# A hybrid decoder block: squares of the tokens without GpSimd, a row of factors spread by products, one value operand in another buffer, two value pieces loaded later

## The chip, the core and the metric

The kernel runs on one core of one Trainium2 chip. The metric is device time in microseconds (us) from start to end of one execution, as the median of several runs. The core has five engines that work side by side, each in the order of its own program: TensorE (PE in the profile; its weight loads are PEld), VectorE (DVE), ScalarE (ACT), GpSimd (POOL) and SyncE (SP), which issues most of the transfers.

## The reference

One decoder block on 2048 tokens of width 1024, all in float32. Cut to what matters:

```python
xn = rmsnorm(h, pre_gain[i])
z = xn @ w_in[i]
q, k, v, fl, g_attn, x_lru, g_lru = jnp.split(z, SPLIT_POINTS, axis=-1)
o_attn = forgetting_attention(q, k, v, fl + b_f[i])          # 8 heads of 128, causal
y_attn = rmsnorm(o_attn, attn_out_gain[i]) * jax.nn.silu(g_attn)
o_lru = rg_lru(causal_depthwise_conv(x_lru, conv_w[i], conv_b[i]), ...)
y_lru = rmsnorm(o_lru, lru_out_gain[i]) * jax.nn.silu(g_lru)
mix = jnp.concatenate([y_attn, y_lru], axis=-1) @ w_out[i]
h = h + rmsnorm(mix, post_gain[i])
e = rmsnorm(p[i] @ w_ple[i], ple_gain[i])                     # per-layer embedding
gate = jax.nn.sigmoid(h @ w_ple_gate[i] + b_ple_gate[i])
h = h + gate * e
```

## The kernel before

Every large product is computed as three products of split operands: a high half (ScalarE copies the source into a rounded type) and a low half (VectorE or GpSimd subtracts the high half from the source). `mm3` (lines 63 to 70) issues high by high, high by low, low by high. The input products are further made by a Strassen-like scheme of seven products on half-size blocks: `XH[i]`, `XL[i]` are the seven token operands, and a `Unit` makes the seven weight operands.

The first third of the program is written as a calendar of slots. `plan(slot, phase, f)` puts a step in a slot; within a slot the phases run in the order LOAD, COMBINE, PREP, JOB, MUL, GATE, STORE, and within a phase in the order of planning. A slot holds about one group of products for TensorE. Since each engine works through its own instructions in order, the calendar fixes what stands behind what on each engine and on the queue of SP.

The opening of the calendar (slots -4 to 30) does this:

- Warming products on a zeroed tile (lines 804 to 808) keep TensorE busy until the first data come.
- The embedding: `ple_load` and `ple_split` bring the per-layer inputs in eight pieces; `embed_mul` makes the 16 tiles of `p @ w_ple`, one tile of twelve products in each of slots 0 to 15; `embed_squares` (ScalarE) sums their squares, and `embed_out` (lines 787 to 796) multiplies each with the row of factors `ple_gain`, held in `pgb` on all 128 partitions. `pgb` is filled by one broadcast load of 512 KB (line 825), which stands in SP's queue between the pieces of tokens. A tile's pair of PSUM banks comes from three such pairs (`bank2`), so tile t needs tile t-3 to be done with.
- The scales of the tokens: `stage_piece` loads the first half of the tokens in eight pieces of 512 KB. `square` (lines 671 to 686) squares them, `add` sums them, `fold` halves the sum, `column_sums` makes sums over partitions by products with ones, `column_roots` takes the roots, `scale_diagonals` and `spread_scales` spread them by a product, and `normalize` multiplies the tokens. There are two groups of 512 tokens, n = 0 and 1. One square of four in each group runs on GpSimd, the others on ScalarE; the additions run on VectorE.
- `plan_operand` splits the token operands, and `differ` makes four of them by subtraction.
- The value unit (begins at slot `VA` = 16, two slots for each of its seven products in the order 0, 5, 1, 2, 3, 4, 6). `plan_weights` (from line 318) gives each of its 14 half operands a buffer out of a ring of five (`op`) and a slot: `sums` (additions and subtractions of weight blocks, on GpSimd), `high` (ScalarE), `low` one slot later in COMBINE (VectorE, for operands 0 and 5 GpSimd), `keep` (stored for the second half of the tokens). The raw weights have a ring of four buffers (`wq`). `plan_v` has the products and what VectorE and ScalarE do with the results.
- At slot `LA` = 30 the units of the recurrent branch begin (their products are the lines with `bank<-XH,op`), and after them the same scheme goes on for some 350 slots in all.

Then attention begins with another calendar: `at(before, slot, f)` and `at(after, slot, f)` place side steps ahead of and behind the work of a slot. In each slot TensorE turns a block of probabilities (`turn_probs`, line 1324), ScalarE and VectorE split it (line 54, line 60), and TensorE multiplies it with the values. Keys and values come in pieces: `load_piece` loads one, `split_piece` splits it on ScalarE and GpSimd. Two value pieces of the first head (numbers 5 and 7, blocks 8 to 15) are loaded at slots 5 and 7 and split at slots 9 and 11; they are first used at slots 27 and 43.

Of the kernel before, what the change touches and what calls it, by code (L numbers as in the profile page):

```python
# [16 lines left out]
P = 128  # L17
# [19 lines left out]
NC = 7  # L37
RAW0 = 5
LOAD, COMBINE, PREP, JOB, MUL, GATE, STORE = range(7)
# [34 lines left out]
def hymba_kernel(ctx: ExitStack, tc: tile.TileContext, x, xT, pT, w_p, w_v, w_o, w_ple, w_pg,  # L74
# [170 lines left out]
    class Unit:  # L245
# [27 lines left out]
        def sums(self, i, hf):  # L273
            n = self.cols
            a11, a12, a21, a22 = self.raws(hf)
            sub = lambda o, x, y: nc.gpsimd.tensor_tensor(out=o, in0=x, in1=y, op=ALU.subtract)
            if i == 1 and self.v or i == 2 and not self.v:
                self.S[1, hf] = wp.tile([P, WT // 2], F32, name="ws", bufs=2)[:, :n]
                nc.gpsimd.tensor_tensor(out=self.S[1, hf], in0=a21, in1=a22, op=ALU.add)
            if i == 2:  # L280
                self.S[2, hf] = self.S[1, hf] if self.v else wp.tile([P, WT // 2], F32, name="ws", bufs=2)[:, :n]
                sub(self.S[2, hf], self.S[1, hf], a11)
            elif i == 3:
                sub(self.S[2, hf], a12, self.S[2, hf])
            elif i == 4:
                sub(a21, a11, a21)
# [5 lines left out]
        def high(self, i, hf):  # L292
            n = self.cols
            op = wp.tile([P, WT], F32R, name="op", bufs=NOP)
            nc.scalar.activation(op[:, :n], self.source(i, hf), AF.Copy)  # L295
            self.ops[i, hf] = op[:, :n], op[:, n:2 * n], op
# [17 lines left out]
    def plan_weights(u, lead=4):  # L314
# [4 lines left out]
        for i in u.prep:  # L319
            for hf in halves:  # L320
                end = u.use(i) + u.halves - 1
                s = max(op_ring.free(), u.use(i) - lead)
                if i == (1 if u.v else 2):
                    s = max(s, ws_ring.ends[-1] + 2 if ws_ring.ends else s)
                op_ring.take(s, end)
                if u.use(i) - s < 2:
                    print("late operand", u.kind, u.h, i, hf, u.use(i) - s)
                starts[i, hf] = s
                if i in (1, 2, 3, 4):
                    plan(s - 1, PREP, lambda i=i, hf=hf: u.sums(i, hf))  # L330
                plan(s, PREP, lambda i=i, hf=hf: u.high(i, hf))
                plan(s + 1, COMBINE, lambda i=i, hf=hf: u.low(i, hf))
                plan(min(s + 2, end), STORE, lambda i=i, hf=hf: u.keep(i, hf))
            if i == 3:
                ws_ring.take(s, s + 1)
        for n in range(4 if u.v else 2):
# [10 lines left out]
            if min(users) - s < 2:  # L347
                print("late raw", u.kind, u.h, n, min(users) - s)
            plan(s, LOAD, lambda n=n: u.load_raw(n))

    fetched = [0]
# [318 lines left out]
    def square(p, n, c, eng):  # L670
# [12 lines left out]
        else:  # L683
            nc.gpsimd.tensor_tensor(out=o, in0=src, in1=src, op=ALU.mult)
        if c:
            plan(now[0] + (1 if eng == "act" else 2), COMBINE, lambda: add(a, a, o))

# [99 lines left out]
    def embed_out(tb):  # L787
        eo = E["o", tb] = (te.tile([P, D], F32, name="eo", bufs=3) if 4 <= tb % 7 else
                           v_tile(("u1", "u5", "o11", "o12", "", "", "", "u1", "o11", "u5", "o12",
                                   "", "", "", "u5", "o12")[tb])[:, :D])  # L790
        b, n = flat(tb), 512 if tb >= RAW0 else 0
        if n:
# [12 lines left out]
    nc.vector.memset(warm, 0.0)  # L805
    b = sbank()
    for _ in range(16):
        nc.tensor.matmul(b, lhsT=warm[:, :P], rhs=warm, start=True, stop=True)
    open_stage("sgA")
    open_right("vpA", vp)  # L810
    plan(-4, LOAD, lambda: ple_load(0))
    for j in range(2):
# [3 lines left out]
    plan(-3, LOAD, lambda: ple_load(1))  # L816
    plan(-3, LOAD, lambda: ple_load(2))
    for n in range(2):
        for kh in range(2):
            if (n, kh) == (1, 0):  # L820
                plan(-2, LOAD, lambda: ple_load(3))
            for k in (0, 2):
                plan(n - 3, LOAD, lambda n=n, kh=kh, k=k: stage_piece(0, n, kh, k))
            if n == 0 and kh == 0:
                plan(-3, LOAD, lambda: nc.sync.dma_start(out=pgb, in_=rows[1:2, :].broadcast_to([P, D])))
    plan(-3, PREP, lambda: ple_split(0))
# [10 lines left out]
    plan(60, JOB, embed_roots)  # L837
    for n, when in enumerate(((0, 1, 1, 2), (3, 3, 4, 5))):
        for c in range(4):
            plan(when[c], JOB, lambda n=n, c=c: square(0, n, c, "pool" if c == 1 else "act"))  # L840
        plan(3 + 3 * n, JOB, lambda n=n: fold(0, n))
# [10 lines left out]
    for k in (0, 2):  # L852
        for i, t in ((1, 13), (2, 16), (4, 19), (6, 21)):
            plan(t + k // 2, JOB, lambda i=i, k=k: differ(i, k, 2, nc.vector))
# [9 lines left out]
    plan_operand(4, 22, "dve")  # L864
    plan_operand(6, 24, "dve")

# [548 lines left out]
    for n, (h, g) in enumerate(stages):  # L1415
        at(before, max(t0[n] - 4, t0[n - 1] + 10) if n else t0[n] + 1, lambda h=h, g=g, n=n: load_gate(h, g, units[n]))
    for p_, a in ((5, 9), (7, 11)):
        at(before, a - 4, lambda p_=p_: load_piece(0, p_))
        at(after, a, lambda p_=p_: split_piece(0, p_))
# [405 lines left out]
    def plan_gate(n):  # L1825
# [67 lines left out]
        plan(s - 2, LOAD, load_e)  # L1893
        if n >= RAW0:
            plan(s + 1, JOB, lambda: tt(u.et[:, :512], u.et[:, :512], G_.egain, ALU.mult))
# [88 lines left out]
```

## Time and profile before

| | us |
|---|---|
| median of three runs | 2088.6 |
| lowest, highest run | 2084.8, 2089.59 |
| the profiled execution | 2089.28 |
| its span | 2087.5 |
| TensorE busy | 2066.8 (99%) |
| VectorE busy | 1620.8 (78%) |
| ScalarE busy | 1148.1 (55%) |
| GpSimd busy | 714.3 (34%) |

Times in the trace count from the start of the span. A line of a timeline has the start, the duration, the engine, the line of the kernel, the operation, `out<-in` by the program's names, the shapes, and in brackets how long the engine stood idle before it and what ended that. TensorE's matmuls overlap, so the distance between two starts counts, not the duration. The clock column (PEclk) is the share of TensorE's full clock that was granted. The opening lies at 0 to 107 us, attention begins near 1046 us.

### The profile page before, as it was taken

How to read it: one execution, taken by the hardware profiler on the slowest of the kernel's cores; microseconds unless marked ns; L12 is line 12 of the kernel's file. 1: busy time of each engine (PE TensorE's matmuls, PEld its weight loads, DVE VectorE, ACT ScalarE, POOL GpSimd, SP SyncE). 2: the span in 40 equal slices, each digit the busy share in tenths (PEclk: the TensorE clock that was granted, in tenths of full speed). 3: DMA queues.
4: the chain of work that ended last, by engine and by line, in shares of the span. 5: the costliest groups of instructions: out<-in, count | busy, mean ns of one | idle time of the engine just before them, and what ended most of it. 6: DMA issues, size and time to landing. Idle time of an engine off the chain costs nothing.

```text
span 2087.5 us, 31241 instructions
## 1 busy us (share of the span) xinstructions
PE 2066.8 (99%) x10602; PEld 1745.4 (84%) x10602; DVE 1620.8 (78%) x2674; ACT 1148.1 (55%) x1839; POOL 714.3 (34%) x617
## 2 busy tenths in 40 slices
PE   9999999999999999999999999999999999999999
PEld 6988888888988898888878888888888888888887
DVE  7977988696759877986378888888885778776676
ACT  6536765344337776874167767777773444452232
POOL 4534555333013335633035665666541000000000
PEclk9999999999999999999999999999999999999999
DMA  8598998987898898779758767777643887665553
GB/s 334 205 331 297 316 348 300 374 313 289 274 279 276 277 274 288 257 251 333 237 183 235 239 215 218 233 231 241 195 149 128 285 254 228 190 218 180 178 174 118
DMA packets 254816, 519.15 MB, mean 249 GB/s; under 512 B 24880, under 2 KB 91712, under 8 KB 254656
## 3 DMA queue, kind: packets, MB, share of 16 engines
q1 hardware_dynamic: 254512, 517.11, 75.5%
q8 instruction: 83, 1.36, 0.3%
q14 instruction: 77, 0.63, 0.1%
q10 hardware_dynamic: 144, 0.05, 0.0%
HBM read 314.81 MB, written 202.25 MB: 248 GB/s over the span
## 4 chain that ended last, share of the span: by engine, by line
PE 91%; DVE 4%; DMA 2%; ACT 1%; issue 1%; SPq 0%; POOL 0%; DVEq 0%; ACTq 0%; POOLq 0%
PE bank L70 15%; PE bank L69 15%; PE bank L68 15%; PE pbank L70 7%; PE pbank L68 7%; PE pbank L69 7%; PE tbank L1324 5%; PE sbank L68 3%; PE sbank L70 3%; PE sbank L69 3%; PE obank L69 3%; PE obank L70 3%; PE obank L68 2%; DMA kvf<-v_d 1%; PE bank L1851 1%
## 5 line engine op out<-in xcount | busy, mean ns | idle before, releaser
L68 PE MATMUL bank<-XH,op 128*128 128x512 f32 x876 | 342.2, 391 | 0.0
L70 PE MATMUL bank<-XH,op 128*128 128x512 f32 x876 | 340.9, 389 | 0.0
L69 PE MATMUL bank<-XL,op 128*128 128x512 f32 x876 | 340.8, 389 | 0.0
L368 DVE TENSOR_TENSOR c<-bank,c 128x512 f32<-128x512 f32 x280 | 186.4, 684 | 109.6 <-PE bank L70 98.4
L60 DVE TENSOR_TENSOR tl<-tbank,th 128x512 fp32r<-128x512 f32 (+1 forms) x320 | 192.4, 607 | 87.1 <-ACT th L54 83.7
L54 ACT ACTIVATE th<-tbank 128x512 fp32r<-128x512 f32 (+1 forms) x320 | 167.7, 530 | 113.0 <-PE tbank L1324 103.7
L69 PEld LDWEIGHTS bank<-XL,op 128*128 128x128 f32 x876 | 164.5, 188 | 34.5 <-issue 0.5
L68 PEld LDWEIGHTS bank<-XH,op 128*128 128x128 f32 x876 | 164.5, 188 | 34.3 <-issue 0.5
L70 PEld LDWEIGHTS bank<-XH,op 128*128 128x128 f32 x876 | 164.5, 188 | 34.0
L1296 ACT ACTIVATE pr<-pr,m 128x1152 f32<-128x1152 f32 (+7 forms) x120 | 148.0, 1233 | 42.2 <-DVE m L1287 41.5
L1324 PE MATMUL tbank<-ident,pr 128*128 128x128 f32 x1062 | 167.3, 273 | 0.0
L152 POOL TENSOR_TENSOR rsm<-rs,mhalf 128x1 f32<-128x1 f32 x16 | 8.7, 543 | 431.5 <-DVE rs L151 431.5
L1324 PEld LDWEIGHTS tbank<-ident,pr 128*128 128x128 f32 x1062 | 130.6, 140 | 27.5
L68 PE MATMUL sbank<-kh,qh 128*128 128x512 f32 (+3 forms) x320 | 136.1, 425 | 2.2 <-DVE m L1287 1.2
L68 PE MATMUL obank<-th,vh 128*128 128x512 f32 (+1 forms) x320 | 123.5, 386 | 0.8 <-ACT th L54 0.8
L295 ACT ACTIVATE op<-wq 128x512 fp32r<-128x512 f32 (+1 forms) x96 | 60.1, 630 | 114.5 <-PE bank L70 79.8
L69 PE MATMUL obank<-tl,vh 128*128 128x512 f32 (+1 forms) x320 | 118.0, 369 | 1.4 <-DVE tl L60 1.1
L70 PE MATMUL obank<-th,vl 128*128 128x512 f32 (+1 forms) x320 | 116.9, 365 | 0.0
L70 PE MATMUL sbank<-kh,ql 128*128 128x512 f32 (+3 forms) x320 | 116.6, 364 | 0.3 <-DVE ql L1227 0.2
L69 PE MATMUL sbank<-kl,qh 128*128 128x512 f32 (+3 forms) x320 | 115.6, 361 | 0.0
L69 PE MATMUL bank<-op,XH 128*128 128x258 f32 x328 | 94.6, 288 | 2.5 <-DVE op L301 2.4
L70 PE MATMUL bank<-op,XL 128*128 128x258 f32 x328 | 95.5, 291 | 0.0
(350 smaller groups left out, 5783.0 us busy)
## 6 DMA issues: line engine op xcount, KB each, us to landing
wo_d<-op SPq DMA_DIRECT2D x140, 512.0 KB, 5.7
op<-wo_d SPq DMA_DIRECT2D x79, 512.0 KB, 5.8
wr<-wo_d SPq DMA_DIRECT2D x61, 512.0 KB, 5.9
wq<-in_w_p_dram SPq DMA_DIRECT2D x40, 512.0 KB, 6.2
vo_d<-op SPq DMA_DIRECT2D x28, 516.0 KB, 3.4
wst<-wt_d SPq DMA_DIRECT2D x56, 256.0 KB, 3.6
wst<-in_w_o_dram SPq DMA_DIRECT2D x40, 256.0 KB, 3.5
X<-xr_d SPq DMA_DIRECT2D x32, 257.5 KB, 3.9
```

What stands on the lines that cost most here:

```text
L54: nc.scalar.activation(hi, src, AF.Copy)
L60: eng.tensor_tensor(out=lo, in0=src, in1=f32(hi), op=ALU.subtract)
L68: nc.tensor.matmul(out, lhsT=wh, rhs=xh, start=start, stop=False)
L69: nc.tensor.matmul(out, lhsT=wh, rhs=xl, start=False, stop=False)
L70: nc.tensor.matmul(out, lhsT=wl, rhs=xh, start=False, stop=stop)
L152: nc.gpsimd.tensor_tensor(out=o, in0=t, in1=mhalf[:, :n], op=ALU.pow)
L295: nc.scalar.activation(op[:, :n], self.source(i, hf), AF.Copy)
L368: nc.vector.tensor_tensor(out=o, in0=x, in1=y, op=ALU.add)
L1296: nc.scalar.activation(pr[0][:, :L], pr[0][:, :L], AF.Exp, bias=m2, scale=-1.0, accum_out=u.r4[:, i:i + 1])
L1324: nc.tensor.transpose(b[:, i * P:(i + 1) * P], u.P[i][:, sb * P:(sb + 1) * P], ident)
L1851: nc.tensor.transpose(b[:, k * P:(k + 1) * P], u.xt[:, kk * P:(kk + 1) * P], ident)
```

## The change

- One square of four in each group of tokens goes from GpSimd to VectorE, and two squares and one addition move by a slot.
- The broadcast load of the factors is gone. GpSimd clears `pgb`, one row of it is loaded by ScalarE's queue, two products with a square of ones spread it, and VectorE copies the result back into `pgb`. There are 9 warming products in place of 16. Two loads of per-layer inputs stand later in SP's queue.
- In the value unit, the subtractions for operands 3 and 4 go from GpSimd to VectorE; the second half of operand 4 lies in a buffer of the raw ring (`wq`) instead of the operands' ring; and `low` of operands 2, 3, 4, 6 stands directly behind `high`. Differences of token operands 4 and 6 and the split of operand 6 stand one slot later.
- The value pieces 5 and 7 of the first head are loaded at slots 9 and 17 and split at slots 15 and 23.
- `RAW0` becomes a range with the same members.

```diff
@@ -35,7 +35,7 @@
 NC = 7
-RAW0 = 5
+RAW = range(5, 16)
 LOAD, COMBINE, PREP, JOB, MUL, GATE, STORE = range(7)
...
@@ -273,7 +273,8 @@
             a11, a12, a21, a22 = self.raws(hf)
-            sub = lambda o, x, y: nc.gpsimd.tensor_tensor(out=o, in0=x, in1=y, op=ALU.subtract)
+            eng = nc.vector if self.begin == VA and i in (3, 4) else nc.gpsimd
+            sub = lambda o, x, y: eng.tensor_tensor(out=o, in0=x, in1=y, op=ALU.subtract)
             if i == 1 and self.v or i == 2 and not self.v:
...
@@ -291,7 +292,8 @@
             n = self.cols
-            op = wp.tile([P, WT], F32R, name="op", bufs=NOP)
+            op = (wp.tile([P, WT], F32R, name="wr", tag="wq", bufs=NRAW) if (self.begin, i, hf) == (VA, 4, 1) else
+                  wp.tile([P, WT], F32R, name="op", bufs=NOP))
             nc.scalar.activation(op[:, :n], self.source(i, hf), AF.Copy)
...
@@ -319,17 +321,20 @@
                 end = u.use(i) + u.halves - 1
-                s = max(op_ring.free(), u.use(i) - lead)
+                sixth = (u.begin, i, hf) == (VA, 4, 1)
+                s = starts[4, 0] if sixth else max(op_ring.free(), u.use(i) - lead)
                 if i == (1 if u.v else 2):
                     s = max(s, ws_ring.ends[-1] + 2 if ws_ring.ends else s)
-                op_ring.take(s, end)
+                if not sixth:
+                    op_ring.take(s, end)
                 if u.use(i) - s < 2:
...
                 plan(s, PREP, lambda i=i, hf=hf: u.high(i, hf))
-                plan(s + 1, COMBINE, lambda i=i, hf=hf: u.low(i, hf))
+                first = u.begin == VA and i not in (0, 5, 1)
+                plan(s if first else s + 1, PREP if first else COMBINE, lambda i=i, hf=hf: u.low(i, hf))
                 plan(min(s + 2, end), STORE, lambda i=i, hf=hf: u.keep(i, hf))
...
@@ -347,6 +352,8 @@
             plan(s, LOAD, lambda n=n: u.load_raw(n))
+        if u.begin == VA:
+            wq_ring.take(starts[4, 1], u.use(4) + 1)
 
...
@@ -681,9 +688,9 @@
         else:
-            nc.gpsimd.tensor_tensor(out=o, in0=src, in1=src, op=ALU.mult)
+            nc.vector.tensor_tensor(out=o, in0=src, in1=src, op=ALU.mult)
         if c:
-            plan(now[0] + (1 if eng == "act" else 2), COMBINE, lambda: add(a, a, o))
+            plan(now[0] + 1 + (p == n == 0 and c == 3), COMBINE, lambda: add(a, a, o))
 
...
@@ -788,7 +795,7 @@
                                    "", "", "", "u5", "o12")[tb])[:, :D])
-        b, n = flat(tb), 512 if tb >= RAW0 else 0
+        b, n = flat(tb), 512 if tb in RAW else 0
         if n:
...
@@ -803,26 +810,29 @@
     nc.vector.memset(warm, 0.0)
-    b = sbank()
-    for _ in range(16):
-        nc.tensor.matmul(b, lhsT=warm[:, :P], rhs=warm, start=True, stop=True)
     open_stage("sgA")
     open_right("vpA", vp)
+    nc.gpsimd.memset(pgb, 0.0)
+    nc.scalar.dma_start(out=pgb[0:1, :], in_=rows[1:2, :])
+    b = sbank()
+    for _ in range(9):
+        nc.tensor.matmul(b, lhsT=warm[:, :P], rhs=warm, start=True, stop=True)
+    E["g"] = bank2()
+    for j in range(2):
+        nc.tensor.matmul(E["g"][:, j], lhsT=sg[1], rhs=pgb[:, j * 512:(j + 1) * 512], start=True, stop=True)
+    plan(0, JOB, lambda: nc.vector.tensor_copy(pgb, E.pop("g").rearrange("p a b -> p (a b)")))
     plan(-4, LOAD, lambda: ple_load(0))
...
     plan(-3, LOAD, lambda: ple_load(1))
-    plan(-3, LOAD, lambda: ple_load(2))
     for n in range(2):
         for kh in range(2):
-            if (n, kh) == (1, 0):
-                plan(-2, LOAD, lambda: ple_load(3))
+            if n:
+                plan(-2, LOAD, lambda kh=kh: ple_load(2 + kh))
             for k in (0, 2):
                 plan(n - 3, LOAD, lambda n=n, kh=kh, k=k: stage_piece(0, n, kh, k))
-            if n == 0 and kh == 0:
-                plan(-3, LOAD, lambda: nc.sync.dma_start(out=pgb, in_=rows[1:2, :].broadcast_to([P, D])))
     plan(-3, PREP, lambda: ple_split(0))
...
@@ -835,9 +845,9 @@
     plan(60, JOB, embed_roots)
-    for n, when in enumerate(((0, 1, 1, 2), (3, 3, 4, 5))):
+    for n, when in enumerate(((0, 1, 1, 1), (3, 4, 4, 5))):
         for c in range(4):
-            plan(when[c], JOB, lambda n=n, c=c: square(0, n, c, "pool" if c == 1 else "act"))
+            plan(when[c], JOB, lambda n=n, c=c: square(0, n, c, "dve" if c == 1 else "act"))
         plan(3 + 3 * n, JOB, lambda n=n: fold(0, n))
...
@@ -850,7 +860,7 @@
     for k in (0, 2):
-        for i, t in ((1, 13), (2, 16), (4, 19), (6, 21)):
+        for i, t in ((1, 13), (2, 16), (4, 20), (6, 22)):
             plan(t + k // 2, JOB, lambda i=i, k=k: differ(i, k, 2, nc.vector))
...
@@ -862,7 +872,7 @@
     plan_operand(4, 22, "dve")
-    plan_operand(6, 24, "dve")
+    plan_operand(6, 25, "dve")
 
...
@@ -1414,8 +1424,8 @@
         at(before, max(t0[n] - 4, t0[n - 1] + 10) if n else t0[n] + 1, lambda h=h, g=g, n=n: load_gate(h, g, units[n]))
-    for p_, a in ((5, 9), (7, 11)):
-        at(before, a - 4, lambda p_=p_: load_piece(0, p_))
+    for p_, a in ((5, 15), (7, 23)):
+        at(before, a - 6, lambda p_=p_: load_piece(0, p_))
         at(after, a, lambda p_=p_: split_piece(0, p_))
...
@@ -1891,7 +1901,7 @@
         plan(s - 2, LOAD, load_e)
-        if n >= RAW0:
+        if n in RAW:
             plan(s + 1, JOB, lambda: tt(u.et[:, :512], u.et[:, :512], G_.egain, ALU.mult))
```

## The prediction

> **What bounds the kernel now.** I read the page first, then TensorE's waits, then the windows and the timelines of the two places that the waits name.
>
> ```profile
> span 2087.5 us, 31241 instructions
> PE 2066.8 (99%) x10602; PEld 1745.4 (84%) x10602; DVE 1620.8 (78%) x2674; ACT 1148.1 (55%) x1839; POOL 714.3 (34%) x617
> ```
>
> TensorE is busy for 99% of the span, so only three things can move the end: TensorE's own work, its pauses, and its clock. The waits of the whole run (engine, line, waited for: us in total, times, longest) are few:
>
> ```profile
> PE sbank L696 <- DVE sq L368: 3.2, 1, 3.2
> PE bank L69 <- DVE op L301: 2.4, 1, 2.4
> PE tbank L1324 <- DVE tl L60: 1.6, 1, 1.6
> ```
>
> The first two lie in the opening, before 107 us, the third at the start of attention. Each was followed by a stretch of half clock. The windows show it (stretch, its length, busy time of PE, PEld, DVE, ACT and POOL, PEclk, DMA share, GB/s): the first two rows are the stretches behind the two pauses of the opening, the third is the pause in attention itself, the fourth the stretch behind it.
>
> ```profile
> 25.10:31.90 6.80, 6.80 (x20) 5.45 (x20) 6.70 (x8) 0.60 (x1) 1.94 (x1) 0.50 0.97 350
> 89.95:93.35 3.40, 3.40 (x19) 3.40 (x18) 3.33 (x5) 0.00 (x0) 2.32 (x2) 0.50 0.82 325
> 1066.20:1069.50 3.30, 1.25 (x7) 0.57 (x5) 1.86 (x3) 3.01 (x6) 1.27 (x1) 1.00 0.01 4
> 1069.60:1072.95 3.35, 3.27 (x8) 2.59 (x9) 3.21 (x10) 2.20 (x4) 2.29 (x2) 0.50 0.55 106
> ```
>
> At a clock of 0.50, 6.8, 3.4 and 3.4 us do half their work: 3.4, 1.7 and 1.7 us are lost. The third row shows how small a pause is enough: 3.30 - 1.25 = 2.05 us idle. The Trainium skill (TensorE: Matmul & The Clock Gate, Part 1: The HAM clock gate) puts the fall to half clock after at least one idle window of some 3.4 us; this row disagrees, and the row decides.
>
> TensorE's own timeline gives the marks for the sum: first embedding product, fifth tile (it waits for a bank), column sums, spread product of the scales, the value unit's pause, first product behind the value unit:
>
> ```profile
> 6.14 0.58 PE L68 MATMUL bank<-wph,ph 128*128 128x512 f32 x1
> 18.30 0.47 PE L68 MATMUL bank<-wph,ph 128*128 128x512 f32 x1 [0.20 <-ACT sq L682]
> 24.51 1.36 PE L696 MATMUL sbank<-onesq,sq 128*128 128x1 f32 x8 [3.21 <-DVE sq L368]
> 34.18 1.02 PE L712 MATMUL sbank<-c,onesq 128*128 128x512 f32 x2
> 89.10 0.39 PE L69 MATMUL bank<-op,XH 128*128 128x258 f32 x1 [2.37 <-DVE op L301]
> 107.40 0.39 PE L68 MATMUL bank<-XH,op 128*128 128x512 f32 x1
> ```
>
> And three rows for prices: a product at full clock in the chain (0.23 us; a tile's twelve make 2.7), TensorE's load waits for the embedding's weights, and a small bank wait.
>
> ```profile
> 32.28 0.23 PE bank L68
> PEld bank L69 <- DVE wpl L60: 1.1, 3, 0.4
> 61.73 0.39 PE L68 MATMUL bank<-op,XH 128*128 128x258 f32 x1 [0.23 <-DVE eo L794]
> ```
>
> **The opening up to the fold.** The chain ahead of the column sums is on VectorE and on the loads:
>
> ```profile
> 13.45 1.22 DVE L794 TENSOR_TENSOR u<-bank,pgb 128x1024 f32<-128x1024 f32 x1 [4.31 <-DMA pgb<-in_rows_dram]
> 18.07 6.38 DVE L368 TENSOR_TENSOR sq<-sq 128x1024 f32<-128x1024 f32 x3
> 35.24 2.06 DVE L717 SCALAR_TENSOR_TENSOR s<-s,vec,sbank 128x512 f32<-128x512 f32 x3 [1.09 <-PE sbank L712]
> 52.98 0.69 DVE L301 TENSOR_TENSOR op<-ws,op 128x516 fp32r<-128x516 f32 x1
> 67.21 1.21 DVE L726 TENSOR_TENSOR s<-s,s 128x1024 f32<-128x1024 f32 x1
> 82.76 2.32 DVE L726 TENSOR_TENSOR s<-s,s 128x1024 f32<-128x1024 f32 x1
> 86.13 2.30 DVE L726 TENSOR_TENSOR s<-s,s 128x1024 f32<-128x1024 f32 x1
> 88.36 0.68 DVE L301 TENSOR_TENSOR op<-ws,op 128x516 fp32r<-128x516 f32 x1
> ```
>
> ```profile
> 14.70 1.06 ACT L682 ACTIVATE sq<-s 128x1024 f32<-128x1024 f32 x1 [1.90 <-DMA s<-in_xT_dram]
> 1.00 0.20 POOL L120 MEMSET cmask<- 128x128 f32 x1
> 12.03 1.90 POOL L684 TENSOR_TENSOR sq<-s 128x1024 f32<-128x1024 f32 x1 [1.33 <-DMA s<-in_xT_dram]
> 19.81 1.89 POOL L684 TENSOR_TENSOR sq<-s 128x1024 f32<-128x1024 f32 x1 [1.16 <-DVE sq L368]
> 85.09 2.27 POOL L276 TENSOR_TENSOR wq<-wq 128x516 f32<-128x516 f32 x1
> ```
>
> The same difference on VectorE takes 1.21 us alone and 2.30 us beside a GpSimd operation (85.09 to 87.36). So each GpSimd operation beside VectorE's costs VectorE about 1.1 us. The three sums at 18.07 took 6.38 us where two of 1.2 and a half one of 0.7 make 3.1; the square at 19.81 lies in them. The Trainium skill (SBUF — State Buffer, Who interferes with whom) says so too, and against this change: a square on VectorE has two SBUF inputs and is itself held up by GpSimd's next split. I charge that from the rows.
>
> Loads: the factors landed at 13.45 and the next piece of tokens at 14.70, so 512 KB takes 1.25 us. The broadcast (512 KB) goes, and one 256 KB load of per-layer input moves behind the first four pieces (estimate: 0.9 us, between half of 1.25 and the whole). The second piece then lands at 12.03 - 0.9 = 11.1, the third at 14.70 - 1.25 - 0.9 = 12.5, the fourth at 13.8.
>
> VectorE, in its new order, from 11.1: square 1.2, output 0 1.2, two additions 2.4, output 1 1.2, third addition 1.2, fold 0.7: 19.0, and with one GpSimd split beside it 20.1. TensorE's fifth tile ends about 20.8 (18.30 plus twelve products of 0.23, less its 0.2 to 0.35 of wait). So the column sums start near 20.8 in place of 24.51, their pause is gone, and so is the gated stretch of 6.8 us.
>
> What the spread of the factors adds: a memset of 128x1024 on GpSimd (128 columns take 0.20, so at most 1.6, more likely 1.1), one row by ScalarE's queue, two products on TensorE and a copy out of PSUM on VectorE. The nearest load is this:
>
> ```profile
> vec<-in_vecs_dram ACTq DMA_DIRECT2D x1, 44.5 KB, 1.9
> pgb<-in_rows_dram SPq DMA_DIRECT2D x1, 512.0 KB, 7.5
> ```
>
> Issued near 3, the row lands between 4.9 and 10.5; I take 5.3, since it has its own queue, as vec has. The products cost 1.7 us (two passes each; the pair at 34.18 holds TensorE for 0.86), so the embedding starts at 7.0 in place of 6.14. That is hidden: TensorE waits 1.1 us for the embedding's weights, and a start 0.9 later only shortens those waits. The copy (1.2) lies in the 4.31 us that VectorE now waits. Nine warming products in place of sixteen end near 4.9: they cover the time until the row comes, and no more.
>
> **From the fold to the value unit.** From 20.1 VectorE does output 2, the second square (2.3 with a split beside it), output 3, two additions, output 4 and the diagonal: 1.2 + 2.3 + 1.2 + 2.4 + 1.2 + 0.7 and 0.1 of roots = 9.1, so the spread product can start at 29.2. TensorE reaches it at 20.8 + 0.8 + two tiles of 2.7 = 27.0: a new pause of some 2 us, in place of one of 3.2, and a lead of 34.18 - 29.2 = 5.0. Then addition, fold and output 5 (2.6): the normalizing starts at 31.8 in place of 35.24, a lead of 3.4.
>
> From 35.24 to the end of the operand that TensorE waited for (88.36 + 0.68) VectorE now takes 53.8 us. Off it: two differences of 2.3 move behind that operand (operands 4 and 6 a slot later): 4.6. On it: four differences of the value weights from GpSimd, 0.7 each: 2.8. Off it again: those four no longer slow VectorE; two of them lay beside the differences already counted, so 2.2. That makes 49.8: operand ready at 81.6. TensorE by itself gets there at 89.1 - 2.4 - 5.0 - 0.2 = 81.5. The two balance, and the value unit goes on at 81.6 in place of 89.1: 7.5 us. The gated stretch behind that pause goes too: 1.7. I take back 1.3 for a bank of the value unit that VectorE releases late near 88 (its additions of slot 24 now follow the moved differences). Opening: **7.9 us**. Bounds: 4 (VectorE's lead of 3.4 and little else) and 11.5 (every pause gone, 3.2 + 3.4 + 2.4 + 1.7 and 0.8 of small ones).
>
> The new buffer for one half operand and the earlier low halves change no work; they only move VectorE's instructions ahead in its order, inside the 49.8. `RAW` holds the same tiles as before: nothing.
>
> **Attention.**
>
> ```profile
> 1050.63 0.60 PE L1324 MATMUL tbank<-ident,pr 128*128 128x128 f32 x4
> 1057.20 1.63 SPq L1176 DMA_DIRECT2D kvf<-v_d  x2
> 1066.49 0.63 ACT L54 ACTIVATE vh<-kvf 128x512 fp32r<-128x512 f32 x1 [4.03 <-DMA kvf<-v_d]
> 1067.64 0.69 DVE L60 TENSOR_TENSOR tl<-tbank,th 128x512 fp32r<-128x512 f32 x1 [3.79 <-ACT th L54]
> 1068.39 0.66 PE L1324 MATMUL tbank<-ident,ph 128*128 128x128 f32 x4 [1.60 <-DVE tl L60]
> 1069.68 0.79 PE L68 MATMUL sbank<-kh,qh 128*128 128x512 f32 x1 [0.64 <-DVE m L1287]
> ```
>
> ScalarE stands 4.03 us before the split of a value piece, and the copies of the turned probabilities are queued behind it. So VectorE stands, and then TensorE. Split at slot 15 in place of 9, the piece is asked for by ScalarE some 12 us later (slots 4 to 12 lie between 1050.63 and 1068.39, so about 2 us each); it lands at 1066.5 as now, since its load waits on the queue, and is there in time. First used at slot 27 (43 for the other): no price. Gain: 1.6, 0.6 and the gated 1.7 = 3.9; I take **3.7**, bounds 0 and 4.5.
>
> **Sum.** 7.9 + 3.7 = 11.6 us. The profiled execution took 2089.28 (span 2087.5 and 1.8 around it) and would take 2077.7; the median is 2088.6, so 2077.0.
>
> **The rivals.**
> First, VectorE eats most of the lead: the four differences bring no relief, the operand comes at 85, the pause and its gated stretch stay in part. Opening 4.5, total 8.2: 2080.4. For it: VectorE's fold chain leads by only 3.4. Chance 0.18.
> Second, every pause of the opening goes: 11.5 + 3.9: 2073.2. For it: VectorE's slots hold under 2.7 us of work in most of the embedding. Chance 0.12.
> Third, the spread's pause of 2 us gates the clock (2.05 did at 1066): TensorE loses 1.7 and is then the later of the two: 2078.7. By the skill's rule of a whole idle window it never would, and the forecast stands. Chance 0.10.
> Fourth, the attention edit only moves the wait to slot 15: 2080.7. Against it: 12 us of room. Chance 0.05.
> Fifth, slower: VectorE is the bound from the first square on and nothing is hidden. Two squares at 2.3, four differences at 1.4, the copy at 1.2 make 11.4; less 4.6, and the longer pause before 89.1 gates a second stretch, 1.7: +8.5, less 3.7 in attention: 2093.4. It decides if the fold ends after 24 us. Chance 0.05.
> Sixth, the row lands near 10.5: the embedding starts 5 us late, TensorE idles into half clock, the opening gives nothing: 2084.9. Chance 0.06.
>
> **How the numbers follow.** The forecast keeps 0.44. About 0.2% (4 us) is what a measurement of this kernel can tell from no change. Below 2084.4 lie the forecast and the first four rivals, 0.89; I take off 0.04, since the three runs of before span 4.8 us: faster 0.85, same 0.10, slower 0.05. The range takes in the second and first rivals and stops short of the sixth: 2072 to 2083.5.
>
> **What would show it.** Column sums near 21 with no wait, clock 1.00 from 5 to 100 us; a wait of 1 to 2 us before the spread product; the value unit's wait for L301 under 1 us; first product behind the value unit near 99.5; no wait of ScalarE for kvf near 1066. I am wrong if TensorE's first wait is for the factors' row, if the value unit's pause stays above 2 us, or if ScalarE waits for a value piece at a later slot.

## The result and the profile after

The changed kernel takes 2078.28 us (median of five runs, 2077.34 to 2078.6), the kernel before 2087.07 (median of five, 2084.8 to 2089.59). The ratio is 0.9956 with a 95% interval of 0.9941 to 0.997: 8.8 us faster. The profiled execution took 2077.34. First the page of the kernel after, its span and busy times:

```profile
span 2075.6 us, 31233 instructions
PE 2058.7 (99%) x10599; PEld 1739.8 (84%) x10599; DVE 1621.4 (78%) x2681; ACT 1148.5 (55%) x1839; POOL 701.0 (34%) x612
```

Its waits of TensorE over the whole run (engine, line, waited for: total us, times, longest). The three of before (3.2, 2.4, 1.6) are gone; the waits for banks that the value unit holds (first two lines), for the diagonals of the scales and for the row of factors are new:

```profile
PE bank L68 <- DVE o L375: 1.5, 1, 1.5
PE bank L68 <- DVE u L375: 1.5, 2, 0.9
PE sbank L719 <- DVE c L712: 1.0, 1, 1.0
PE bank L822 <- DMA pgb<-in_rows_dram: 0.6, 1, 0.6
```

TensorE's timeline of the kernel after, at the marks of the prediction: the row's products, the first embedding product, the fifth tile, the column sums (no bracket: no wait), the spread product, the product that before waited at 89.10 (again no bracket), two late banks, and the first product behind the value unit.

```profile
5.77 1.96 PE L822 MATMUL bank<-pgb,onesq 128*128 128x512 f32 x4 [0.56 <-DMA pgb<-in_rows_dram]
7.16 0.79 PE L68 MATMUL bank<-wph,ph 128*128 128x512 f32 x1
19.39 0.47 PE L68 MATMUL bank<-wph,ph 128*128 128x512 f32 x1 [0.16 <-DVE u L801]
22.29 0.95 PE L703 MATMUL sbank<-onesq,sq 128*128 128x1 f32 x8
29.83 1.12 PE L719 MATMUL sbank<-c,onesq 128*128 128x512 f32 x2 [0.99 <-DVE c L712]
81.29 0.28 PE L69 MATMUL bank<-op,XH 128*128 128x258 f32 x1
87.32 0.36 PE L68 MATMUL bank<-op,XH 128*128 128x258 f32 x1 [0.58 <-DVE u L375]
91.96 0.39 PE L68 MATMUL bank<-op,XH 128*128 128x258 f32 x1 [1.46 <-DVE o L375]
102.04 0.47 PE L68 MATMUL bank<-XH,op 128*128 128x512 f32 x1 [0.88 <-DVE u L375]
```

VectorE in the kernel after: the first square, the fold, the normalizing, the low half that TensorE waited for in the kernel before, and the two low halves that follow the moved differences:

```profile
13.29 1.23 DVE L691 TENSOR_TENSOR sq<-s 128x1024 f32<-128x1024 f32 x1 [1.92 <-DMA s<-in_xT_dram]
19.16 2.48 DVE L375 TENSOR_TENSOR sq<-sq 128x1024 f32<-128x1024 f32 x2
32.16 2.05 DVE L724 SCALAR_TENSOR_TENSOR s<-s,vec,sbank 128x512 f32<-128x512 f32 x3
79.93 0.68 DVE L303 TENSOR_TENSOR op<-ws,op 128x516 fp32r<-128x516 f32 x1
87.82 3.48 DVE L303 TENSOR_TENSOR op<-wq,op 128x516 fp32r<-128x516 f32 x2
```

GpSimd beside that last row, which makes weight sums for the first recurrent unit at the same time:

```profile
87.42 1.63 POOL L280 TENSOR_TENSOR ws<-wq 128x512 f32<-128x512 f32 x1 [14.93 <-DMA wq<-in_w_p_dram]
89.13 1.62 POOL L277 TENSOR_TENSOR ws<-ws,wq 128x512 f32<-128x512 f32 x1
```

Where the time came from, by marks that both profiled executions share:

| TensorE starts | before | after | lead |
|---|---|---|---|
| the value unit's product that waited | 89.10 | 81.29 | 7.8 |
| first product behind the value unit | 107.40 | 102.04 | 5.4 |
| first turning of attention | 1050.63 | 1045.27 | 5.4 |
| a block behind the two value pieces | 1099.68 | 1089.88 | 9.8 |
| the end of attention | 1605.32 | 1593.40 | 11.9 |

The opening gave 5.4 us and the start of attention 4.4. The last 2.1 built up in the later heads, which the change doesn't touch: before took 505.6 us for the last stretch of the table, after 503.5, and the kernels below between 503.6 and 506.2, in no order that goes with their edits. So the two profiles differ by 11.9 us and the medians by 8.8.

The table is one pair of executions. In the other traces the first product behind the value unit starts at 101.70 (after_again) and 100.88 (open_only) with the opening of the change, and at 106.81 (att_only) and 107.36 (split_late) with the opening of before: by this mark the opening gives 4.8 to 6.5 us.

### The profile page after: what moved, and what is told of

The parts are those of the page before. It is cut to its first block, busy times and chain, and to the rows that moved or that the text cites. A ratio compares the mean times of both kernels' runs of the same rounds, so it can differ in the third digit from the quotient of the medians.

```text
span 2075.6 us, 31233 instructions
## 1 busy us (share of the span) xinstructions
PE 2058.7 (99%) x10599; PEld 1739.8 (84%) x10599; DVE 1621.4 (78%) x2681; ACT 1148.5 (55%) x1839; POOL 701.0 (34%) x612
## 4 chain that ended last, share of the span: by engine, by line
PE 91%; DVE 4%; DMA 2%; ACT 1%; issue 1%; SPq 0%; POOL 0%; DVEq 0%; ACTq 0%; POOLq 0%
PE bank L70 15%; PE bank L68 15%; PE bank L69 15%; PE pbank L70 7%; PE pbank L68 7%; PE pbank L69 7%; PE tbank L1334 5%; PE sbank L68 3%; PE sbank L70 3%; PE sbank L69 3%; PE obank L69 3%; PE obank L70 3%; PE obank L68 3%; PE bank L1861 1%; PE tbank L1353 1%
## 5 line engine op out<-in xcount | busy, mean ns | idle before, releaser
L69 PE MATMUL bank<-XL,wr 128*128 128x512 f32 x244 | 94.9, 389 | 0.0
L68 PE MATMUL bank<-XH,wr 128*128 128x512 f32 x244 | 94.9, 389 | 0.0
```

What stands on the lines that cost most here:

```text
L68: nc.tensor.matmul(out, lhsT=wh, rhs=xh, start=start, stop=False)
L69: nc.tensor.matmul(out, lhsT=wh, rhs=xl, start=False, stop=False)
```

## The experiments

The theory at the outset was the prediction's: the opening gives the larger part, since VectorE's chain up to the value unit is shorter and TensorE's pauses go, and attention gives the rest, since ScalarE no longer stands before a value piece. The rivals: one of the parts does it all; or TensorE's half clock was the loss, whatever VectorE does; or it was the loads. Each median below stands beside runs of the kernel before on the same chip. The ratio goes by all runs and not by the two medians, so a gain read from it can differ from the difference of the medians by over 1 us.

| kernel | us (lowest to highest, runs) | ratio to before, 95% |
|---|---|---|
| att_only | 2083.99 (2082.19 to 2085.37, 11) | 0.9983, 0.9974 to 0.9992 |
| open_only | 2081.25 (2079.29 to 2084.09, 7) | 0.9974, 0.9963 to 0.9984 |
| no_value | 2081.0 (2078.58 to 2082.59, 6) | 0.9971, 0.9959 to 0.9983 |
| bcast | 2076.82 (2075.39 to 2077.61, 5) | 0.995, 0.9938 to 0.9963 |
| gpsq | 2080.08 (2078.58 to 2082.44, 7) | 0.997, 0.9959 to 0.9981 |
| split_late | 2085.29 (2083.93 to 2087.55, 11) | 0.999, 0.9981 to 0.9999 |
| l0dve | 2076.45 (2075.16 to 2078.55, 5) | 0.995, 0.9938 to 0.9963 |
| low6 | 2077.8 (2077.7 to 2079.93, 5) | 0.9959, 0.9946 to 0.9971 |
| fill | 2086.71 (2083.79 to 2089.5, 11) | 0.9994, 0.9985 to 1.0003 |
| after_again | 2078.48 (2075.63 to 2079.91, 5) | 0.9953, 0.994 to 0.9965 |
| l0dve_2 | 2076.21 (2075.27 to 2079.4, 5) | 0.9946, 0.9932 to 0.9959 |
| bcast_l0dve | 2075.92 (2074.66 to 2077.47, 5) | 0.9943, 0.993 to 0.9955 |

The first four ran beside a before of 2086.9, the next four beside 2088.06, the last four beside 2087.67.

### The two halves: att_only and open_only

att_only is the kernel before with the attention edit alone:

```diff
-    for p_, a in ((5, 9), (7, 11)):
-        at(before, a - 4, lambda p_=p_: load_piece(0, p_))
+    for p_, a in ((5, 15), (7, 23)):
+        at(before, a - 6, lambda p_=p_: load_piece(0, p_))
```

> The kernel before with the attention edit alone (pieces 5 and 7 loaded at slots 9 and 17, split at 15 and 23). Theory A, the two parts add up: the opening stays as before (first product behind the value unit at 107.4 us), ScalarE does not wait for a value piece near 1066, the clock stays at 1.00 there, and the time falls by 4.4 us (slot for slot the attention marks of the changed kernel gained 9.8 - 5.4): 2082.7. Rival B, the wait only moves to a later slot: ScalarE waits for a value piece at slot 15 or 23, and the time stays at 2087. Rival C, the further 2 us that the later heads of attention gained belong to this edit: 2080.5.

open_only is the changed kernel with those lines put back:

```diff
-    for p_, a in ((5, 15), (7, 23)):
-        at(before, a - 6, lambda p_=p_: load_piece(0, p_))
+    for p_, a in ((5, 9), (7, 11)):
+        at(before, a - 4, lambda p_=p_: load_piece(0, p_))
```

> The changed kernel with the attention edit undone. Theory A: first product behind the value unit at 102.0 us, ScalarE waits some 4 us for a value piece near 1061 and TensorE falls to half clock for 3.4 us: 2087.1 - 5.4 = 2081.7. Rival B: the opening's lead is eaten by that wait, since the piece lands at a time that depends on the queue and not on the opening: the wait grows to 8 or 9 us and the time is 2086 to 2087.

Attention alone gives 2.9 us by the medians (3.5 by the ratio, where 4.4 was expected), the opening alone 5.65; together 8.55, and the whole change gives 8.8. The two parts add up and neither does it all. ScalarE's row in open_only shows the wait that the attention edit removes:

```profile
1059.26 0.63 ACT L54 ACTIVATE vh<-kvf 128x512 fp32r<-128x512 f32 x1 [3.64 <-DMA kvf<-v_d]
```

TensorE's rows of open_only show what it costs there: two waits, 1.86 us in all. TensorE's clock stayed at 1.00 behind them, against the expectation, where the kernel before lost a further 1.7 to half clock:

```profile
1061.15 0.66 PE L1334 MATMUL tbank<-ident,ph 128*128 128x128 f32 x4 [1.22 <-DVE tl L60]
1062.45 0.51 PE L68 MATMUL sbank<-kh,qh 128*128 128x512 f32 x1 [0.64 <-DVE m L1297]
```

### Attention: the place or the load? split_late

The kernel before, with the splits at slots 15 and 23 but the loads left at slots 5 and 7:

```diff
-    for p_, a in ((5, 9), (7, 11)):
-        at(before, a - 4, lambda p_=p_: load_piece(0, p_))
+    for p_, a in ((5, 15), (7, 23)):
+        at(before, a - (10, 16)[p_ // 7], lambda p_=p_: load_piece(0, p_))
```

> The kernel before with only the splits of the value pieces 5 and 7 moved (slots 15 and 23), their loads where they were (slots 5 and 7). Theory A, what stands in the way is ScalarE's place in the order and not the load: no wait of ScalarE for a value piece, the same as with the attention edit alone: 2084.0 (2087 - 2.9). Rival B, the loads' place matters too, since two loads ahead of the others hold up the biases: a wait elsewhere near 1060, and 2085.5 to 2087.

2.8 us by the medians, as much as att_only's 2.9 (by the ratios 2.1 and 3.5, with intervals that overlap), and no wait of ScalarE for the pieces. The traces agree. From the first turning of attention to the block of the table's fourth row TensorE takes 49.1 us in before, 47.0 in open_only, 45.2 in att_only and 44.3 in split_late. So it is the split's place in ScalarE's order; asking later for the load adds nothing that shows.

### Parts of the opening: no_value, gpsq, bcast

no_value is the changed kernel with the edits of the value unit undone: the weight differences back on GpSimd, operand 4's second half back in the ring, the low halves a slot later, the differences of the tokens at their old slots:

```diff
-            sub = lambda o, x, y: eng.tensor_tensor(out=o, in0=x, in1=y, op=ALU.subtract)
+            sub = lambda o, x, y: nc.gpsimd.tensor_tensor(out=o, in0=x, in1=y, op=ALU.subtract)
...
-            op = (wp.tile([P, WT], F32R, name="wr", tag="wq", bufs=NRAW) if (self.begin, i, hf) == (VA, 4, 1) else
-                  wp.tile([P, WT], F32R, name="op", bufs=NOP))
+            op = wp.tile([P, WT], F32R, name="op", bufs=NOP)
...
-                plan(s if first else s + 1, PREP if first else COMBINE, lambda i=i, hf=hf: u.low(i, hf))
+                plan(s + 1, COMBINE, lambda i=i, hf=hf: u.low(i, hf))
...
-        for i, t in ((1, 13), (2, 16), (4, 20), (6, 22)):
+        for i, t in ((1, 13), (2, 16), (4, 19), (6, 21)):
...
```

> The changed kernel with the edits of the value unit undone (subtractions for operands 3 and 4 on GpSimd again, all half operands in the operands' ring, low halves a slot after the high ones, token operands 4 and 6 at their old slots); squares, spread and attention as changed. Theory A: the normalizing still starts at 32.2 in place of 35.2, but GpSimd's subtractions slow VectorE's differences as before (1.2 to 2.3 us), TensorE pauses 2 us or more before value product 3 and the clock is gated for 3.4 us; first product behind the value unit at 104.5 to 105, time 2081. Rival B, the value edits are worth nothing, all comes from the squares: 102 and 2078.3. Rival C, the value edits cost, through the low halves of operand 6 that took 3.48 us in the changed kernel: 100.5 and 2076.8.

2.7 us slower than the change by the medians, and its first product behind the value unit is 2.4 later (104.41 for 102.04). TensorE waits for the operand again; the product starts at 84.58, where the change has 81.29 and before 89.10:

```profile
84.58 0.39 PE L69 MATMUL bank<-op,XH 128*128 128x258 f32 x1 [2.37 <-DVE op L301]
```

The half clock that was expected behind it did not come: the clock stayed at 1.00.

gpsq is the changed kernel with one square of four back on GpSimd, and the squares and additions at the old slots:

```diff
-            nc.vector.tensor_tensor(out=o, in0=src, in1=src, op=ALU.mult)
+            nc.gpsimd.tensor_tensor(out=o, in0=src, in1=src, op=ALU.mult)
...
```

> The changed kernel with the squares as before: one of four on GpSimd again, in the old slots, its addition two slots later. Theory A, the squares are the larger part of the opening's gain: GpSimd's squares hold up VectorE's additions again (1.2 us become 1.7 to 3), the column sums wait 1 to 3 us, the normalizing starts at 34 to 35 in place of 32.2, first product behind the value unit at 104 to 105, time 2081. Rival B, the earlier loads alone did it: column sums without a wait and 102, 2078.3. Rival C, without the squares VectorE is lighter by 2.3 us and the value unit's late banks come earlier: 100.5, 2077.

1.8 us slower than the change by the medians. But it ran beside the slowest before of all: against that it gains 8.0, where the change gains 8.8. By the marks it loses 0.8, with the first product behind the value unit at 102.85, where 104 to 105 was expected. So the squares are worth 0.8 to 1.8, and are not the larger part. The column sums wait again, for half as long as before:

```profile
23.34 1.05 PE L703 MATMUL sbank<-onesq,sq 128*128 128x1 f32 x8 [1.59 <-DVE sq L375]
```

bcast is the changed kernel with the 512 KB broadcast of the factors and the sixteen warming products back:

```diff
-    nc.gpsimd.memset(pgb, 0.0)
-    nc.scalar.dma_start(out=pgb[0:1, :], in_=rows[1:2, :])
...
+            if n == 0 and kh == 0:
+                plan(-3, LOAD, lambda: nc.sync.dma_start(out=pgb, in_=rows[1:2, :].broadcast_to([P, D])))
```

> The changed kernel with the factors by one broadcast load again (512 KB between the second and the third piece of tokens) and 16 warming products; no row load, no spreading products, no copy. Theory A: the third and fourth pieces land 1.25 us later, VectorE's fold ends about 1.2 us later, and the spread of the scales (29.8 in the changed kernel) starts at 31.0: first product behind the value unit at 103, time 2079.3. Rival B, the spread by products is worth nothing because it also makes the embedding start a microsecond later: 102.0 and 2078.3. Rival C, the broadcast is what held the squares: the pause before the column sums and the gated stretch come back, 105 or later and 2081.5.

It loses nothing that can be told: 2076.82 beside the change's 2078.28, with intervals that overlap. The fifth tile does wait for its bank, since the factors come later, but that second is hidden (the first product behind the value unit starts at 101.42, in the change at 102.04):

```profile
19.97 0.47 PE L68 MATMUL bank<-wph,ph 128*128 128x512 f32 x1 [1.03 <-DVE u L801]
```

So of the opening's 5.65 us, the value unit's edits carry the most, 2.4 to 2.7, and the squares 0.8 to 1.8, each as the loss when it alone is undone; the spread by products carries none. What is left is not assigned: the order of the loads was not tested by itself, nor were the value unit's edits taken apart.

### Was the half clock the loss? fill

The kernel before, with three more float32 products into the sum bank ahead of the column sums. Their results are overwritten; they only keep TensorE busy.

```diff
+        if p == n == 0:
+            for _ in range(3):
+                nc.tensor.matmul(b, lhsT=sg[1], rhs=s[0, 0][:, 0], start=True, stop=True)
```

> The kernel before with three products of ones with a piece of the tokens (float32, about 0.86 us each) put ahead of the first column sums, into the bank that the column sums then overwrite; they compute nothing that is used. They fill 2.6 of the 3.2 us in which TensorE waits there, and move nothing else. Theory A, half of what that pause costs is the clock: column sums at 24.5 as before, but no half clock from 25 to 32, the spread product of the scales at 31 to 32 in place of 34.2; since VectorE stands behind at the value unit, 1 to 3 us of it reach the end: 2084.5, and the runs lie closer together. Rival B, the half clock there is hidden, because VectorE sets when the value unit goes on: 2087.5.

By the time, nothing that can be told from no change (0.9985 to 1.0003). Yet the pause shrank from 3.21 to 0.66 us and TensorE's clock stayed at 1.00 from 5 to 88 us. TensorE's rows of fill, column sums and value unit:

```profile
25.27 1.05 PE L699 MATMUL sbank<-onesq,sq 128*128 128x1 f32 x8 [0.66 <-DVE sq L368]
87.60 0.39 PE L69 MATMUL bank<-op,XH 128*128 128x258 f32 x1 [2.86 <-DVE op L301]
```

VectorE's normalizing in fill starts where it did before (35.24):

```profile
35.21 2.05 DVE L720 SCALAR_TENSOR_TENSOR s<-s,vec,sbank 128x512 f32<-128x512 f32 x3
```

TensorE got back 3.4 us of half clock and 2.6 of a pause, and at the value unit it waits longer (2.86 for 2.37). Its first product behind the value unit starts at 105.90, which is 0.9 to 1.5 us earlier than in the three traces with the opening as before. So of some 6 us that TensorE got back, at most 1.5 got past the value unit: VectorE's chain sets that place. The first pause and its half clock were, by themselves, cheap.

### The late banks: l0dve, low6, l0dve_2

The prediction charged 1.3 us for late banks behind the value unit's wait; the change loses more there. The suspect is GpSimd, which makes the sums at 87.42 and 89.13 just when VectorE makes two low halves. l0dve moves the two sums to VectorE:

```diff
-            eng = nc.vector if self.begin == VA and i in (3, 4) else nc.gpsimd
+            eng = nc.vector if self.begin == VA and i in (3, 4) or self.begin == LA and i == 2 else nc.gpsimd
...
-                nc.gpsimd.tensor_tensor(out=self.S[1, hf], in0=a21, in1=a22, op=ALU.add)
+                eng.tensor_tensor(out=self.S[1, hf], in0=a21, in1=a22, op=ALU.add)
```

> The changed kernel with the two weight sums of the first recurrent unit (operand 2) on VectorE instead of GpSimd. In the changed kernel two low halves on VectorE took 3.48 us at 87.8 while GpSimd made these sums (87.4 to 90.7), and TensorE then waited 1.46 us for a bank. Theory A, it is the meeting of the two engines: VectorE takes on two operations of 0.7 and loses a hold-up of 2.2, the wait of 1.46 shrinks to about 0.6, first product at 101, time 2077.3. Rival B, VectorE has simply too much to do there: the wait grows to 2 or more, 103, 2079.5. Rival C, the wait is not on the path, since the next wait (0.88 before the first recurrent product) stays: 102.0, 2078.3.

VectorE's row of l0dve for the same two low halves, 1.30 us for 3.48:

```profile
87.64 1.30 DVE L303 TENSOR_TENSOR op<-wq,op 128x516 fp32r<-128x516 f32 x2
```

The wait of 1.46 is gone, here that of 0.58 too, and TensorE is behind the value unit at 100.17 for 102.04:

```profile
100.17 0.47 PE L68 MATMUL bank<-XH,op 128*128 128x512 f32 x1 [0.88 <-ACT op L297]
```

low6 instead takes the low halves of operand 6 off VectorE and gives them to GpSimd:

```diff
-            eng = nc.gpsimd if self.begin == VA and i in (0, 5) else nc.vector
+            eng = nc.gpsimd if self.begin == VA and i in (0, 5, 6) else nc.vector
```

> The changed kernel with the low halves of value operand 6 on GpSimd (idle from 72 to 87 us there) instead of VectorE. Theory A (the meeting of the two engines): VectorE is rid of two operations that took 3.48 us; GpSimd's new ones, about 1.5 each near 81 and 84, meet two of VectorE's operations with two SBUF inputs and cost 1.1 each; the wait of 1.46 shrinks to under 0.5, first product at 101, time 2077.2. Rival B (too much work on VectorE) expects the same and more: all three late waits of 2.9 us together go, 99.3, 2075.5. Rival C: GpSimd's operations meet VectorE's on the path to operand 4, a new pause of over 1 us before value product 4: 103, 2079.5.

No gain that can be told: 2077.8. The same engines meet a little earlier: GpSimd needs 4.38 us for the two halves (its row is at the end), and the low half of a token operand that VectorE makes beside them takes 2.31, where it takes 1.22 in the change (first row the change, second low6):

```profile
84.22 1.22 DVE L741 TENSOR_TENSOR XL<-s,XH 128x1024 fp32r<-128x1024 f32 x1
84.26 2.31 DVE L741 TENSOR_TENSOR XL<-s,XH 128x1024 fp32r<-128x1024 f32 x1
```

The wait has only moved:

```profile
88.46 0.36 PE L68 MATMUL bank<-op,XH 128*128 128x258 f32 x1 [1.43 <-DVE u L375]
```

l0dve_2 is l0dve once more, beside after_again, the changed kernel as it is.

> The changed kernel with the two weight sums of the first recurrent unit on VectorE, once more, beside the changed kernel on one chip. Theory: faster than that by the 1.8 us that its first recurrent product came earlier: 2076.5. Rival: no difference, 2078.3.

> The changed kernel itself, on the chip of the runs beside it, for comparison: 2078.3, and again within 1.5 us from run to run, since none of its pauses is long enough to gate the clock.

2076.21 against 2078.48 on one chip; the first l0dve had 2076.45. The runs of the two overlap, though, and those of after_again spread over 4.3 us, not the 1.5 that was expected. In l0dve_2's trace the wait of 1.46 us is gone again, while one of 0.58 is there, which after_again's lacks: that one comes and goes with the run. The traces say it more sharply. From the start of the normalizing to the first product behind the value unit it takes 69.7 to 70.1 us with the meeting (after, after_again, open_only), and 68.4 and 68.1 without (l0dve, l0dve_2); with the old broadcast it takes 68.6 with the meeting (bcast) and 67.4 without (bcast_l0dve, the next kernel). So the meeting cost 1.2 to 2.0 us; the medians (1.8 and 2.3) fit that but do not show it by themselves.

### The best version: bcast_l0dve

The changed kernel with both edits, the old broadcast and the two sums on VectorE.

> The changed kernel with the factors by one broadcast load and 16 warming products as before, and with the two weight sums of the first recurrent unit on VectorE. Theory, the spread by products is worth nothing and the sums on VectorE 1.8: 2075 to 2076.5, no slower than with the sums alone. Rival, the broadcast costs its microsecond once the late waits are gone: 2077.5.

2075.92, the lowest median of all; its interval (0.993 to 0.9955) overlaps those of l0dve_2 and after_again. It is 11.8 us under the before of its chip; that it beats l0dve alone isn't shown.

## Why the prediction was right, and where its terms were off

The total came out near 2077.0 and on the predicted side, and the mechanism held: the opening's pauses and ScalarE's wait went, because VectorE's chain got shorter and the split moved in ScalarE's order. That it came out so near is luck in part, as the last point says. Point by point:

**Loads.** The second to fourth pieces were due at 11.1, 12.5 and 13.8; ScalarE and VectorE started on them at 13.29, 14.60 and 15.89. The spacing of 1.3 was right, the start 2 us out: moving a 256 KB load behind them brought the first piece no nearer. It came between 10.74 and 11.87 in the four traces with the old order of loads, between 10.49 and 12.01 in the eight with the new.

**Up to the fold.** The fold ended at 21.6 (predicted 20.1), for that reason; from VectorE's first square on the chain took 8.4 us for 9.0. The column sums began at 22.29 (20.8), TensorE being as late as VectorE: no pause and no half clock, as predicted.

**The spread of the factors.** The row made TensorE wait 0.56 us; its products began at 5.77 (5.3) and held TensorE until 7.16 (7.0). The memset took 0.95 us. All hidden, as forecast, but with bcast level there is no gain in it either. The prediction had named a first wait of TensorE for the factors' row as a sign of being wrong. Behind the warming products that is TensorE's first wait, so the sign came; it was badly chosen, since a wait of 0.56 there cost nothing.

**To the value unit.** Spread product at 29.83 after a wait of 0.99 (29.2 after 2), normalizing at 32.16 (31.8), operand ready at 79.93 + 0.68 = 80.6 (81.6). TensorE came by at 81.29, without a wait, against 81.6: a lead of 7.8 where 7.5 was due. The near hit hides two errors: VectorE began 2.2 us late, and its chain from there to the operand was 3.2 shorter than reckoned (the second square, for one, took 1.68 where 2.3 was charged). no_value and fill back the balance behind this number: with VectorE's work put back TensorE waits 2.37, and speeding TensorE alone brings at most 1.5. The first rival, VectorE eating the lead, is out, and so is the third: the spread's pause was 0.99 and not 2, and the clock stayed at 1.00.

**The term that was mis-sized** is the end of the opening: + 1.7 for the gated stretch, - 1.3 for "a bank of the value unit that VectorE releases late near 88". The stretch did go, but the lead fell from 7.8 to 5.4, so what was lost is 7.8 + 1.7 - 5.4 = 4.1. The three waits make 0.58 + 1.46 + 0.88 = 2.9 of it. Counted from start to start, against the usual 0.12 between two products, the same three stops make 3.4, and a short one at 83.62 another 0.3; the rest is in small delays. The wait of 1.46 comes from VectorE's low halves meeting GpSimd's sums, which l0dve shows; that is the 1.2 to 2.0 us. That of 0.58 comes and goes with the run, and one of 0.88 at the same product is there in l0dve too. The prediction had the price of such a meeting (1.21 against 2.30); it charged it for the new squares and counted where the change takes meetings away, but it didn't ask what would run beside VectorE near 88, once its work there had moved. So the opening gave 5.65 instead of 7.9.

**Attention** gave 2.9 by the medians for 3.7. The 3.9 of the working had 1.7 for half clock in it, which the profiled execution of before had and open_only's did not. The waits alone are 1.9 in open_only and 2.2 in before; that the median lies between the two cases fits a half clock in some runs only. Of the three traces with the old places, before and fill have it there and open_only has not; how often it comes over all runs isn't known.

**The whole.** Two terms 2.2 and 0.8 too large make 3.0. The total still came out within 1.3 us, and that is luck: it was set against a median of 2088.6, which is 1.5 above the 2087.07 of the five runs of before, and the whole gave 0.2 more than the two parts.

## What to carry to other kernels

When work moves in an engine's order, list what will then run beside it on the engines that slow it: a VectorE operation with two SBUF inputs beside a GpSimd operation cost here as much as the work itself. A pause and half clock on the busiest engine are worth only as much as the next join with another engine leaves of them. And a saving taken from one profile that holds a half-clock stretch belongs to that execution; set it as a range for the median.

## What the runs showed of the hardware

**The clock counts in windows, and where a pause lies in them decides.** Apart from the one in which each run ends, all stretches of half clock here begin and end on a grid of 3.413 us, whose start differs from run to run. In before they begin at 25.09, 89.94 and 1069.56 us, which lie 19 and 287 windows apart. So the same pause of 2.37 us is dear or cheap. In the kernel before it lay in one window, and the next ran at 0.50 (windows with their length, busy PE, PEld, DVE, ACT, POOL, clock, DMA share, GB/s):

```profile
86.53:89.94 3.41, 1.04 (x9) 0.84 (x8) 3.41 (x4) 2.17 (x4) 0.83 (x1) 1.00 0.61 210
89.94:93.35 3.41, 3.41 (x19) 3.41 (x18) 3.34 (x5) 0.00 (x0) 2.32 (x2) 0.50 0.83 328
```

In split_late an edge cut the same 2.37 us into 1.60 and 0.77, and the clock stayed at 1.00:

```profile
84.43:87.84 3.41, 1.81 (x15) 1.61 (x13) 3.41 (x3) 2.59 (x4) 2.44 (x2) 1.00 0.62 193
87.84:91.25 3.41, 2.64 (x21) 2.64 (x22) 3.38 (x6) 1.20 (x2) 0.57 (x1) 1.00 0.90 300
```

So 1.60 us idle of 3.41 doesn't bring the clock down, and 2.05 does (the attention of before). In gpsq 3.41 - 1.73 = 1.68 us idle was enough, where the eight sums of one column count as busy though they are small:

```profile
21.56:24.97 3.41, 1.73 (x11) 1.42 (x11) 3.38 (x4) 2.21 (x4) 1.18 (x1) 1.00 1.02 410
24.97:28.38 3.41, 3.41 (x10) 2.67 (x9) 3.31 (x5) 0.00 (x0) 1.94 (x1) 0.50 0.93 294
```

The Trainium skill (TensorE: Matmul & The Clock Gate, Part 1: The HAM clock gate) has the window right: 3413 ns, running freely. Its condition, an idle window, is too strict: about half a window was enough. Over the 14 traces, the run's start and end apart, each of the nine windows with 1.68 us idle or more was followed by half clock, and none with 1.60 or less was. That this is why runs of one kernel differ is likely but not shown: the five of before spread over 4.8 us and the five of after over 1.3, but the five of after_again over 4.3. Why the first pause of before brought two windows of half clock and the same pause of 3.21 in split_late one is open.

**A meeting with GpSimd costs both engines.** VectorE lost 3.48 - 1.30 = 2.2 us on two low halves beside two sums, 1.1 for each, and in low6 2.31 - 1.22 = 1.1 on the low half of a token operand: the price of the prediction's rows held in both places. Where only a part of the operation lay beside GpSimd's it cost less (1.68 - 1.23 = 0.45 for the change's second square). The other side is new: in low6 GpSimd's two low halves took 4.38 us, mostly beside VectorE operations with two SBUF inputs. The same work of another operand takes it 1.30 each in before at 43.38, where the VectorE operations beside it read one input from a bank.

```profile
81.12 4.38 POOL L303 TENSOR_TENSOR op<-wq,op 128x516 fp32r<-128x516 f32 x2 [8.98 <-ACT op L297]
```
